# Seven dense layers take gate, up and the next gate together in their first round

## The chip, the cores and the metric

The kernel runs on one core of a Trainium2 chip. A core has a matrix engine (TensorE, PE in the profile, with its weight loads as PEld), VectorE (DVE), ScalarE (ACT), GpSimd (POOL) and SyncE (SP), which issues the loads of weights. The metric is the device time of one execution in microseconds, the median of several runs: 3132.03 us for the kernel before (three runs, 3131.13 to 3134.92).

## The reference, cut to what matters

A model of several kinds of blocks on 256 tokens of 1024 features, with 16 more tokens put in front in one of the blocks. Around the blocks' mixers stand dense layers of this form; the second kind of block has the same gate, up and down without the norm in front, and layer norms behind:

```python
def rmsnorm(x, g):
    xf = x.astype(jnp.float32)
    y = xf * lax.rsqrt(jnp.mean(xf * xf, -1, keepdims=True) + EPS)
    return (y * g.astype(jnp.float32)).astype(x.dtype)

def macaron_half_ffn(x, pre_g, post_g, w_gate, w_up, w_down):
    h = rmsnorm(x, pre_g)
    h = (jax.nn.silu(h @ w_gate) * (h @ w_up)) @ w_down
    return x + 0.5 * rmsnorm(h, post_g)
```

w_gate and w_up are 1024 x 2816, w_down is 2816 x 1024. The change touches the first two products alone.

## The kernel before, in words

x lies with features on the partitions: 8 slices k of 128 features by n tokens. Every operand is split into a high part and a remainder (xh and xl, wh and wl), and a product is three matmuls: xh by wh, xl by wh, xh by wl (`mm3p`, profile lines 594 to 596).

**Weights.** `Mat.get` (lines 222 to 238) brings a block of weights, 1024 rows by 256 columns, in two pieces of 128 x 1024 elements. A piece is loaded on SP's queue into one of 6 raw buffers, cast by ScalarE into one of 5 wh buffers (line 237), and subtracted by VectorE into one of 5 wl buffers (line 238). A buffer comes free when TensorE has done its last matmul with the piece before it. A block makes 48 matmuls: 8 slices k, two halves of 128 columns, three products.

**The dense layer.** `ffn` (line 518 on) splits x (`split_x`, lines 270 and 271, slice by slice as the layer before makes it), and goes through 11 column blocks c. Block c takes a gate block and an up block. For c = 0 both go together, slice by slice, 12 matmuls for each k; later blocks do gate first, then up. With n up to 256, gate c and up c each have one PSUM buffer of the pool `acc`, which has four; so gate 2 takes the buffer of gate 0. `glu` multiplies gate by the norm's factor rb (line 602, VectorE, which reads the gate's buffer for the last time), takes silu on ScalarE (line 603), and multiplies by up (line 607).

**The norm.** As the scale of a token can be applied behind the product, x goes in without it. The squares of x's slices are taken by ScalarE (line 369) and added by GpSimd (line 363). `rms_wide` (lines 396 to 422) is written behind the loops of c = 0: it splits the sum into th and tl, sums over features with two matmuls (lines 410, 411), and makes rb by rw (line 413), a root on ScalarE (line 415), a reciprocal (417) and three small steps (418 to 420). One layer uses the narrow `rms` instead: a sum into columns (line 295), small steps (lines 336 to 343), a broadcast by TensorE (line 325) and a copy to rb (line 394). `by_tokens` (lines 425 to 433) makes a copy of rw's values for the end of the layer (line 429, two matmuls, and line 432).

**The end of a layer.** `add_norm` (line 783) or `layer_norm` (line 860) sums squares over features (line 295), takes the root (`inv_sqrt`, lines 328 to 345, isv to isc), broadcasts it (line 325) and makes the next x slice by slice (t at line 794, x at line 795). `hold_weights` (line 347) keeps the root and its last step in mind; `Mat.get` counts its calls in `held`, and the call at which the count is 0 is issued behind those two. With two calls free, the first four pieces of the next layer (gate 0 and up 0) may go ahead of the root, and the fifth goes behind it.

**What sets the order.** Each engine runs its instructions in its own order, and a scheduler puts them there from the program's order, its dependences and its own estimate of times. So the order on an engine is not the order of the program text; it is shown below where the change moves it.

Seven layers have n up to 256 and no work given as `first`. They are called layers 1 to 7 here, in order of time. Layers 1, 2, 3 and 7 use `rms_wide`; layers 4 and 5, in the second block, have no norm in front; layer 6 uses the narrow `rms`, over 272 tokens.

Of the kernel before, what the change touches and what calls it, by code (L numbers as in the profile page):

```python
# [20 lines left out]
KD = D // 128  # L21
# [150 lines left out]
def parts_tile(p, name, k, n, dtype=F32R, **kw):  # L172

    return p.tile([128, k, (n + 63) // 64 * 64], dtype, name=name, **kw)[:, :, :n]
# [68 lines left out]
class Ops(Net):  # L243
# [274 lines left out]
    def ffn(self, x, n, g, wg, wu, wd, out, first=None, side=None, stats=None):  # L518

        nc = self.nc
        with self.phase("ffn") as p, ExitStack() as scope:
            px = scope.enter_context(self.phase("ffx", side="right"))
            vt = rb = ahead = wide = None
            if first:
                x.need(0)
                parts = []
                for i, (k, m) in enumerate(((0, 2), (2, 2), (4, 4))):
                    parts.append(wg.get(k, m, 0, 256))  # L530
                    x.need(i + 1)
                ahead = [Pieces(2, [t for q in w for t in (q.tiles[0][:, i:i + 2] for i in range(0, q.each, 2))])
                         for w in zip(*parts)]
                first()
            xh, xl = self.split_x(px, x, n, g)
            hh = parts_tile(p, "hh", FF // 128, n)
            hl = parts_tile(p, "hl", FF // 128, n)
            pair = n <= 256

            def tiles(other=0):  # L540
                if pair:
                    t = self.acc.tile([128, 2, 256], F32, name="acc")
                    return t[:, :, :n], [t[:, m, :n] for m in range(2)]
                t = [(self.acc, self.aux)[m < other].tile([128, 512], F32, name=("acc", "aux")[m < other])[:, None, :n]
                     for m in range(2)]
                return t, [a[:, 0] for a in t]

            def mm(ps, w, k):
                for m in range(2):
                    ms = slice(m * 128, m * 128 + 128)  # L550
                    self.mm3p(ps[m], w[0][:, k, ms], w[1][:, k, ms], xh[:, k], xl[:, k],
                              k == 0 and (m == 0 or not pair), k == KD - 1 and (m == 1 or not pair))

            for c in range(FF // 256):
                cg = ahead if ahead and c == 0 else wg.get(0, KD, c * 256, 256)
                cu = wu.get(0, KD, c * 256, 256)
                tg, pg = tiles(2 * (c == 1))
                tu, pu = tiles(c == 1)
                if c == 0 and not first:
                    for k in range(KD):  # L560
                        mm(pg, cg, k)
                        mm(pu, cu, k)
                else:
                    for k in range(KD):
                        mm(pg, cg, k)
                    for k in range(KD):
                        mm(pu, cu, k)
                if c == 0 and g is not None and n == 256 and stats is None:
                    rb, wide = self.rms_wide(p, x, n)
                elif c == 0 and g is not None:  # L570
                    rt, rb, vt = self.rms(x, stats or n)
                    if side:
                        side.stats = rt, rb
                    rb, vt = rb[:, :n], vt[:, :self.nt(n)]
                    if not pair:
                        self.hold_weights(1)
                if pair:
                    self.glu(p, hh[:, 2 * c:2 * c + 2], hl[:, 2 * c:2 * c + 2], tg, tu, rb, n, 2)
                else:
                    for m in range(2):  # L580
                        i = 2 * c + m
                        self.glu(p, hh[:, i:i + 1], hl[:, i:i + 1], tg[m], tu[m], rb, n, 1)
            o = out(hh[:, FF // 128 - 1, 0:1].bitcast(F32))
            self.out_proj(wd, hh, hl, n, list(range(FF // 128)), o, side=side and (lambda: side.place(px)))
            if side:
                side.scope = scope.pop_all()
            if wide is not None:
                vt = self.by_tokens(wide, n, 1e-6)
            return o, vt
# [2008 lines left out]
```

## Time and profile before

| what | value |
|---|---|
| median of three runs | 3132.03 us |
| the profiled execution | 3120.05 us |
| its span | 3117.8 us |
| mean granted clock of TensorE | 0.979 |
| TensorE busy | 3009.0 us, 97% |
| VectorE busy | 2071.4 us, 66% |
| ScalarE busy | 1527.8 us, 49% |
| GpSimd busy | 324.1 us, 10% |

Busy shares are means over the whole span. TensorE's granted clock is given as a share of its full 2.4 GHz: 0.50 is 1.2 GHz. An idle time in brackets behind an instruction is that of its engine just ahead of it, with what ended it. An instruction's times can overlap with the next one's on TensorE, whose matmuls are pipelined: its pace is read from the starts.

### The profile page before, as it was taken

Reading aid. Unit: us, or ns where it says so; the run is one execution under the profiler, and the core shown is the slowest. Engines: PE = TensorE matmul, PEld = TensorE weight load, DVE = VectorE, ACT = ScalarE, POOL = GpSimd, SP = SyncE. Lnnn points to the kernel's source line nnn. Section 1 sums busy time; section 2 is a strip of 40 time slices with the busy share of each in tenths; the row PEclk is TensorE's granted clock in tenths of the full one; section 3 lists DMA queues with packets and bytes.
Section 4 is the critical chain, followed back from the end, with each engine's and each line's share of the span. In section 5 each row is a group of like instructions: output and inputs, shape, how many; then the busy total and the mean of one; then the engine's idle time right before and its main releaser. Section 6 shows DMA issues by size and latency. Waiting matters only on the chain.

```text
span 3117.8 us, 63347 instructions
## 1 busy us (share of the span) xinstructions
PE 3009.0 (97%) x26260; PEld 2899.6 (93%) x26260; DVE 2071.4 (66%) x3465; ACT 1527.8 (49%) x2418; POOL 324.1 (10%) x379
## 2 busy tenths in 40 slices
PE   8999999999899999999999999999999999999998
PEld 8998999999777899999989999999989999998898
DVE  6578766658867765657886665565566656658764
ACT  5455555545433544546565454454444444444543
POOL 0010101000211100001100110100102001012101
PEclk9999999999999999999999999999999999999999
DMA  7664566665311466765345536555443555662453
GB/s 241 192 190 137 167 188 191 203 201 172 103 36 35 123 192 197 208 191 174 112 135 161 171 118 194 180 155 171 142 129 108 172 170 165 193 196 90 130 192 119
DMA packets 142528, 494.61 MB, mean 159 GB/s; under 512 B 15760, under 2 KB 18448, under 8 KB 141984
## 3 DMA queue, kind: packets, MB, share of 16 engines
q1 hardware_dynamic: 136512, 478.88, 49.8%
q10 hardware_dynamic: 5696, 11.62, 1.1%
q8 instruction: 206, 3.38, 0.4%
q14 instruction: 82, 0.67, 0.1%
q0 software_dynamic: 32, 0.07, 0.0%
HBM read 487.35 MB, written 3.15 MB: 157 GB/s over the span
## 4 chain that ended last, share of the span: by engine, by line
PE 90%; DVE 5%; ACT 2%; POOL 2%; issue 1%; DMA 0%; SPq 0%; POOLq 0%; DVEq 0%; ACTq 0%
PE acc L594 25%; PE acc L595 25%; PE acc L596 25%; PE aux L1430 2%; DVE wl L238 1%; PE aux L295 1%; POOL acc L363 1%; PE aux L325 1%; PE acc L2433 1%; ACT wh L237 1%; PE acc L514 1%; PE acc L515 1%; PE acc L516 1%; PE aux L1450 0%; PE aux L668 0%
## 5 line engine op out<-in xcount | busy, mean ns | idle before, releaser
L238 DVE TENSOR_TENSOR wl<-raw,wh 128x1024 fp32r<-128x1024 f32 (+2 forms) x934 | 1123.9, 1207 | 688.4 <-ACT wh L237 679.1
L237 ACT CAST wh<-raw 128x1024 fp32r<-128x1024 f32 (+2 forms) x934 | 952.3, 1023 | 1091.4 <-PE acc L595 802.1
L594 PE MATMUL acc<-xh,wh 128*128 128x256 f32 (+1 forms) x4464 | 1263.8, 285 | 28.9 <-ACT xh L270 17.0
L595 PE MATMUL acc<-xl,wh 128*128 128x256 f32 (+1 forms) x4464 | 1255.1, 282 | 1.3 <-DVE xl L271 1.3
L596 PE MATMUL acc<-xh,wl 128*128 128x256 f32 (+1 forms) x4464 | 1254.8, 281 | 0.9 <-DVE wl L238 0.9
L594 PEld LDWEIGHTS acc<-xh,wh 128*128 128x128 f32 x4464 | 849.6, 191 | 36.7 <-ACT xh L270 18.4
L595 PEld LDWEIGHTS acc<-xl,wh 128*128 128x128 f32 x4464 | 851.7, 191 | 6.5 <-issue 3.6
L596 PEld LDWEIGHTS acc<-xh,wl 128*128 128x128 f32 x4464 | 850.6, 191 | 3.0 <-DVE wl L238 1.3
L594 PE MATMUL acc<-hh,wh 128*128 128x256 f32 (+1 forms) x1760 | 490.2, 279 | 0.0
L596 PE MATMUL acc<-hh,wl 128*128 128x256 f32 (+1 forms) x1760 | 489.8, 278 | 0.0
L595 PE MATMUL acc<-hl,wh 128*128 128x256 f32 (+1 forms) x1760 | 489.8, 278 | 0.0
L595 PEld LDWEIGHTS acc<-hl,wh 128*128 128x128 f32 x1760 | 330.9, 188 | 0.1
L594 PEld LDWEIGHTS acc<-hh,wh 128*128 128x128 f32 x1760 | 330.6, 188 | 0.1
L596 PEld LDWEIGHTS acc<-hh,wl 128*128 128x128 f32 x1760 | 330.6, 188 | 0.0
L363 POOL TENSOR_TENSOR acc<-so 128x256 f32<-128x256 f32 (+1 forms) x16 | 19.6, 1227 | 1120.0 <-ACT so L779 1119.5
L363 POOL TENSOR_TENSOR acc<-acc,so 128x256 f32<-128x256 f32 (+1 forms) x68 | 80.9, 1189 | 305.9 <-ACT so L779 303.1
L607 DVE TENSOR_TENSOR gv<-acc,glu 128x512 f32<-128x512 f32 (+1 forms) x130 | 77.5, 611 | 47.8 <-PE acc L596 42.0
L595 PE MATMUL acc<-ml,wh 128*128 128x256 f32 x280 | 79.8, 287 | 2.3 <-DVE ml L254 2.3
L602 DVE TENSOR_TENSOR glu<-acc,rb 128x512 f32<-128x512 f32 (+1 forms) x106 | 61.3, 596 | 30.4 <-PE acc L596 30.3
L594 PE MATMUL acc<-mh,wh 128*128 128x256 f32 x280 | 80.6, 290 | 0.9 <-ACT mh L1678 0.8
L596 PE MATMUL acc<-mh,wl 128*128 128x256 f32 x280 | 78.9, 284 | 0.0
L609 DVE TENSOR_TENSOR hl<-gv,hh 128x512 fp32r<-128x512 f32 (+1 forms) x132 | 77.2, 602 | 0.0
(620 smaller groups left out, 3772.8 us busy)
## 6 DMA issues: line engine op xcount, KB each, us to landing
raw<-w SPq DMA_DIRECT2D x880, 512.0 KB, 3.9
raw<-w SPq DMA_DIRECT2D x46, 256.0 KB, 3.1
so<-memT ACTq DMA_DIRECT2D x20, 256.0 KB, 3.8
raw<-w SPq DMA_DIRECT2D x8, 192.0 KB, 2.8
x<-xT SPq DMA_DIRECT2D x4, 256.0 KB, 6.1
mk<-so ACTq DMA_DIRECT2D x4, 256.0 KB, 2.5
mv<-so ACTq DMA_DIRECT2D x4, 256.0 KB, 2.9
mk<-mk ACTq DMA_DIRECT2D x1, 1024.0 KB, 4.8
```

Of the source, the lines that this page charges most:

```text
L237: nc.scalar.copy(h, r)
L238: nc.vector.tensor_sub(l, r, h.bitcast(F32))
L295: self.nc.tensor.matmul(ps[:, j:j + 1], a[:, j * 128:(j + 1) * 128], self.tab["ones"], start=(j == 0 and first), stop=(j == nt - 1 and las ...
L325: self.nc.tensor.matmul(ps[:, j * 128:j * 128 + w], r[:w, j:j + 1].to_broadcast([w, 128]), self.tab["ident"][:w, :w], start=(j == 0), stop ...
L363: self.nc.gpsimd.tensor_add(d, total[1], t)
L594: t.matmul(out, wh, xh, start=first, stop=False, **kw)
L595: t.matmul(out, wh, xl, start=False, stop=False, **kw)
L596: t.matmul(out, wl, xh, start=False, stop=last, **kw)
L602: nc.vector.tensor_mul(s, pg, rb[:, None, :].to_broadcast([128, m, n]))
L607: nc.vector.tensor_mul(v, pu, s)
L609: nc.vector.tensor_sub(hl, v, hh.bitcast(F32))
L1430: nc.tensor.matmul(ps[R[a], c], lhsT(c, a), rhs(c, a), start=first and c == 0, stop=c == 3, skip_group_check=True)
```

## The change

In the seven layers the first round takes three weight blocks, gate 0, up 0 and gate 1, slice by slice: 18 matmuls for each k. Their six pieces are asked for by six calls of `get`, each of half a block (four slices), in the order gate 0, up 0, gate 1, and again. The round for c = 1 then has up 1 alone. From c = 2 on nothing changes. Where `held` is 2, it is set to 5, so that five of the small calls may go ahead of the root. `Pieces` puts the two halves of a block together again.

```diff
--- before.py
+++ after.py
@@ -551,12 +551,32 @@
                     self.mm3p(ps[m], w[0][:, k, ms], w[1][:, k, ms], xh[:, k], xl[:, k],
                               k == 0 and (m == 0 or not pair), k == KD - 1 and (m == 1 or not pair))
 
+            three = pair and not first
+            if three and self.held == 2:
+                self.held = 5
             for c in range(FF // 256):
-                cg = ahead if ahead and c == 0 else wg.get(0, KD, c * 256, 256)
-                cu = wu.get(0, KD, c * 256, 256)
-                tg, pg = tiles(2 * (c == 1))
-                tu, pu = tiles(c == 1)
-                if c == 0 and not first:
+                if three and c == 0:
+
+                    each = [(wg, 0), (wu, 0), (wg, 256)]
+                    got = [[w.get(k, 4, at, 256) for w, at in each] for k in (0, 4)]
+                    both = [[Pieces(4, [a[i].tiles[0], b[i].tiles[0]]) for i in range(2)] for a, b in zip(*got)]
+                    (tg, pg), (tu, pu), ahead1 = [tiles() for _ in range(3)]
+                    for k in range(KD):
+                        for w, ps in zip(both, (pg, pu, ahead1[1])):
+                            mm(ps, w, k)
+                elif three and c == 1:
+                    cu = wu.get(0, KD, 256, 256)
+                    (tg, pg), (tu, pu) = ahead1, tiles()
+                    for k in range(KD):
+                        mm(pu, cu, k)
+                else:
+                    cg = ahead if ahead and c == 0 else wg.get(0, KD, c * 256, 256)
+                    cu = wu.get(0, KD, c * 256, 256)
+                    tg, pg = tiles(2 * (c == 1))
+                    tu, pu = tiles(c == 1)
+                if three and c < 2:
+                    pass
+                elif c == 0 and not first:
                     for k in range(KD):
                         mm(pg, cg, k)
                         mm(pu, cu, k)
```

(Lines behind the change have numbers higher by 20: 602 becomes 622, 794 becomes 814.)

**The sum of the norm, TensorE, layer 1.** In these rows acc with a number is a PSUM buffer in use for one block, xh7 is the last slice of x, xh0 the first, th and tl are the sum of squares. Before, the end of up 0 and the start of gate 1:

```order
L594 MATMUL acc_4173<-xh7_4097,wh_4168 128x256
L595 MATMUL acc_4173<-xl7_4105,wh_4168 128x256
L596 MATMUL acc_4173<-xh7_4097,wl_4169 128x256
L410 MATMUL aux_4298<-th_4294,one_4300 128x256 [waits Activation_49]
L411 MATMUL aux_4298<-tl_4295,one_4300 128x256 [waits DVE_49]
L595 MATMUL acc_4344<-xl0_4098,wh_4322 128x256
L596 MATMUL acc_4344<-xh0_4090,wl_4323 128x256
```

After, the end of gate 1 and the start of up 1:

```order
L614 MATMUL acc_4186<-xh7_4097,wh_4180 128x256
L615 MATMUL acc_4186<-xl7_4105,wh_4180 128x256
L616 MATMUL acc_4186<-xh7_4097,wl_4181 128x256
L410 MATMUL aux_4359<-th_4355,one_4361 128x256 [waits Activation_49]
L411 MATMUL aux_4359<-tl_4356,one_4361 128x256 [waits DVE_49]
L614 MATMUL acc_4393<-xh0_4090,wh_4383 128x256
L615 MATMUL acc_4393<-xl0_4098,wh_4383 128x256
```

The two matmuls of lines 410 and 411 stand behind 96 matmuls of the layer before, and behind 144 after. From line 410 to the first matmul of gate 2 there are 97 rows before and 52 after. That place after, the end of up 1 and the start of gate 2:

```order
L614 MATMUL acc_4393<-xh7_4097,wh_4389 128x256
L615 MATMUL acc_4393<-xl7_4105,wh_4389 128x256
L616 MATMUL acc_4393<-xh7_4097,wl_4390 128x256
L429 MATMUL aux_6352<-tab_all_125,rw_4365 128x1 [waits DVE_49]
L429 MATMUL aux_6352<-tab_all_125,rw_4365 128x1
L614 MATMUL acc_4473<-xh0_4090,wh_4451 128x256 [waits DVE_49,PE_49,Activation_49]
L615 MATMUL acc_4473<-xl0_4098,wh_4451 128x256
```

And before:

```order
L594 MATMUL acc_4345<-xh7_4097,wh_4340 128x256
L595 MATMUL acc_4345<-xl7_4105,wh_4340 128x256
L596 MATMUL acc_4345<-xh7_4097,wl_4341 128x256
L594 MATMUL acc_4473<-xh0_4090,wh_4451 128x256 [waits DVE_49,Activation_49]
L595 MATMUL acc_4473<-xl0_4098,wh_4451 128x256
```

Line 429's two matmuls stood at the end of the layer and now stand ahead of gate 2.

**From the sum to the release of gate 0's buffer, VectorE, layer 1.** wl is a weight piece's subtraction; glu is the multiplication by rb. Before:

```order
L254 TENSOR_TENSOR tl<-acc,th 128x256 [waits Activation_49]
L238 TENSOR_TENSOR wl<-raw,wh 128x1024 [waits DMAHW0_49,PE_49,Activation_49]
L413 TENSOR_SCALAR rw<-aux 128x256 [waits PE_49]
L238 TENSOR_TENSOR wl<-raw,wh 128x1024 [waits DMAHW1_49,Activation_49]
L417 RECIPROCAL rb<-t 128x256 [waits Activation_49]
L238 TENSOR_TENSOR wl<-raw,wh 128x1024 [waits DMAHW2_49,PE_49,Activation_49]
L418 TENSOR_TENSOR t<-rb 128x256 [waits DVE_49]
L419 SCALAR_TENSOR_TENSOR t<-t,rw 128x256 [waits DVE_49]
L420 SCALAR_TENSOR_TENSOR rb<-t,rb 128x256 [waits DVE_49]
L238 TENSOR_TENSOR wl<-raw,wh 128x1024 [waits DMAHW3_49,PE_49,Activation_49]
L602 TENSOR_TENSOR glu<-acc,rb 128x512 [waits DVE_49]
```

After:

```order
L238 TENSOR_TENSOR wl<-raw,wh 128x1024 [waits DMAHW1_49,PE_49,Activation_49]
L413 TENSOR_SCALAR rw<-aux 128x256 [waits PE_49]
L238 TENSOR_TENSOR wl<-raw,wh 128x1024 [waits DMAHW2_49,Activation_49]
L417 RECIPROCAL rb<-t 128x256 [waits Activation_49]
L238 TENSOR_TENSOR wl<-raw,wh 128x1024 [waits DMAHW3_49,DVE_49]
L418 TENSOR_TENSOR t<-rb 128x256 [waits DVE_49]
L238 TENSOR_TENSOR wl<-raw,wh 128x1024 [waits DMAHW4_49,PE_49,Activation_49]
L419 SCALAR_TENSOR_TENSOR t<-t,rw 128x256 [waits DVE_49]
L432 TENSOR_SCALAR rv<-aux 128x2 [waits PE_49]
L420 SCALAR_TENSOR_TENSOR rb<-t,rb 128x256 [waits DVE_49]
L238 TENSOR_TENSOR wl<-raw,wh 128x1024 [waits DMAHW5_49,Activation_49]
L622 TENSOR_TENSOR glu<-acc,rb 128x512 [waits DVE_49]
```

Between rw and the multiplication there were three wl; now there are four, and the small rv (line 432). Between tl and rw there are two wl now, of which the second is shown.

**The start, VectorE, layer 1.** o is the output of the layer before, isv to isc its norm's small steps, t the first step of the new x. Before:

```order
L782 COPY o<-acc 128x512 [waits Activation_49]
L782 COPY o<-acc 128x256 [waits Activation_49]
L238 TENSOR_TENSOR wl<-raw,wh 128x1024 [waits DMAHW4_49,PE_49,Activation_49]
L782 COPY o<-acc 128x256 [waits Activation_49]
L336 TENSOR_SCALAR isv<-aux 128x2 [waits PE_49]
L340 RECIPROCAL isy<-isr 128x2 [waits Activation_49]
L341 TENSOR_TENSOR ist<-isy 128x2 [waits DVE_49]
L342 SCALAR_TENSOR_TENSOR ist<-ist,isv 128x2 [waits DVE_49]
L343 SCALAR_TENSOR_TENSOR isc<-ist,isy 128x2 [waits DVE_49]
L238 TENSOR_TENSOR wl<-raw,wh 128x1024 [waits DMAHW5_49,Activation_49]
L794 SCALAR_TENSOR_TENSOR t<-o,vec,aux 128x256 [waits PE_49]
```

After:

```order
L802 COPY o<-acc 128x512 [waits Activation_49]
L802 COPY o<-acc 128x256 [waits Activation_49]
L238 TENSOR_TENSOR wl<-raw,wh 128x1024 [waits DMAHW4_49,PE_49,Activation_49]
L238 TENSOR_TENSOR wl<-raw,wh 128x1024 [waits DMAHW5_49,PE_49,Activation_49]
L802 COPY o<-acc 128x256 [waits Activation_49]
L336 TENSOR_SCALAR isv<-aux 128x2 [waits PE_49]
L340 RECIPROCAL isy<-isr 128x2 [waits Activation_49]
L341 TENSOR_TENSOR ist<-isy 128x2 [waits DVE_49]
L342 SCALAR_TENSOR_TENSOR ist<-ist,isv 128x2 [waits DVE_49]
L343 SCALAR_TENSOR_TENSOR isc<-ist,isy 128x2 [waits DVE_49]
L814 SCALAR_TENSOR_TENSOR t<-o,vec,aux 128x256 [waits PE_49]
```

The fifth wl stood between isc and t, and stands ahead of the last copy of o and of isv.

## Rows read from the trace of the kernel before

**Rows 1.** The page's parts 1 and 4: busy time by engine; the chain by engine.
```profile
PE 3009.0 (97%) x26260; PEld 2899.6 (93%) x26260; DVE 2071.4 (66%) x3465; ACT 1527.8 (49%) x2418; POOL 324.1 (10%) x379
...
PE 90%; DVE 5%; ACT 2%; POOL 2%; issue 1%; DMA 0%; SPq 0%; POOLq 0%; DVEq 0%; ACTq 0%
```

**Rows 2.** Who TensorE waited for: us in total, times, longest us.
```profile
PE acc L594 <- ACT xh L270: 17.0, 8, 2.4
...
PE acc L595 <- DVE xl L271: 1.3, 3, 0.8
...
PE acc L596 <- DVE wl L238: 0.9, 1, 0.9
```

**Rows 3.** Layer 1's start, stretches: us, PE PEld DVE ACT POOL busy, PEclk, DMA, GB/s.
```profile
337.90:343.80 5.90, 5.86 (x27) 5.86 (x28) 5.90 (x15) 3.90 (x11) 3.87 (x4) 0.50 0.18 71
343.80:351.90 8.10, 8.10 (x74) 8.10 (x73) 6.31 (x9) 4.79 (x9) 2.59 (x3) 1.00 0.20 67
```

**Rows 4.** VectorE in order of time, layer 1's start: start us, us, ..., [idle before].
```profile
333.65 0.15 DVE L336 TENSOR_SCALAR isv<-aux 128x2 f32<-128x2 f32 x1
...
335.00 1.23 DVE L238 TENSOR_TENSOR wl<-raw,wh 128x1024 fp32r<-128x1024 f32 x1 [0.18 <-ACT wh L237]
336.14 0.86 DVE L794 SCALAR_TENSOR_TENSOR t<-o,vec,aux 128x256 f32<-128x256 f32 x2
```

**Rows 5.** TensorE in order of time, layer 1.
```profile
334.88 0.71 PE L325 MATMUL aux<-tab_all,isc 128*128 128x128 f32 x4 [1.28 <-DVE isc L343]
...
337.94 0.80 PE L594 MATMUL acc<-xh,wh 128*128 128x256 f32 x2 [2.35 <-ACT xh L270]
...
351.78 0.28 PE L410 MATMUL aux<-th,one 128*128 128x256 f32 x1
```

**Rows 6.** VectorE in order of time, layer 1, from the norm's sum on.
```profile
353.42 0.42 DVE L413 TENSOR_SCALAR rw<-aux 128x256 f32<-128x256 f32 x1
...
354.88 1.75 DVE L417 RECIPROCAL rb<-t 128x256 f32<-128x256 f32 x1
356.55 1.16 DVE L238 TENSOR_TENSOR wl<-raw,wh 128x1024 fp32r<-128x1024 f32 x1
357.63 0.41 DVE L418 TENSOR_TENSOR t<-rb 128x256 f32<-128x256 f32 x1
...
358.54 0.43 DVE L420 SCALAR_TENSOR_TENSOR rb<-t,rb 128x256 f32<-128x256 f32 x1
358.88 1.22 DVE L238 TENSOR_TENSOR wl<-raw,wh 128x1024 fp32r<-128x1024 f32 x1
360.01 1.28 DVE L602 TENSOR_TENSOR glu<-acc,rb 128x512 f32<-128x512 f32 x2
```

**Rows 7.** ScalarE in order of time, layer 1, a cast.
```profile
357.46 1.05 ACT L237 CAST wh<-raw 128x1024 fp32r<-128x1024 f32 x1 [1.71 <-PE acc L595]
```

**Rows 8.** Stretches elsewhere: idle times of TensorE and what follows them.
```profile
1431.20:1434.50 3.30, 0.34 (x4) 0.14 (x2) 2.89 (x6) 2.94 (x6) 0.00 (x0) 1.00 0.72 218
1436.00:1439.40 3.40, 3.24 (x16) 2.94 (x15) 3.29 (x11) 2.76 (x6) 0.00 (x0) 0.51 0.53 157
1486.60:1489.00 2.40, 0.44 (x5) 0.20 (x3) 2.40 (x5) 0.80 (x2) 0.00 (x0) 1.00 0.67 203
1489.00:1493.00 4.00, 3.85 (x33) 3.65 (x33) 3.96 (x10) 1.77 (x3) 0.00 (x0) 1.00 0.47 136
```

**Rows 9.** VectorE in order of time, starts of layers 5 and 7.
```profile
1840.06 1.23 DVE L238 TENSOR_TENSOR wl<-raw,wh 128x1024 fp32r<-128x1024 f32 x1
...
2918.77 0.16 DVE L336 TENSOR_SCALAR isv<-aux 128x2 f32<-128x2 f32 x1 [1.39 <-PE aux L295]
```

**Rows 10.** TensorE and VectorE in order of time, layer 6.
```profile
2627.37 0.83 PE L295 MATMUL aux<-tab_all,acc 128*128 128x1 f32 x6 [0.99 <-POOL acc L363]
...
2630.77 0.93 PE L325 MATMUL aux<-tab_all,isc 128*128 128x128 f32 x6
...
2631.26 2.36 DVE L238 TENSOR_TENSOR wl<-raw,wh 128x1024 fp32r<-128x1024 f32 x2 [1.62 <-ACT wh L237]
```

## The prediction

> **What bounds the kernel now.** I read the page first: TensorE is busy 97% of the span and makes 90% of the chain of waits [rows 1]. So time moves only where TensorE idles or runs at a lower clock; VectorE and ScalarE have room on average. The second view was the list of who waited for whom on TensorE, to see what the change could win at the starts of the seven layers (numbered 1 to 7 in order of time; 1, 2, 3 and 7 take their norm with the wide sum, 6 with the narrow one, 4 and 5 have none). There are 17.0 us of waits for the first slice of x, 8 of them, 1.3 us for its low part, and 0.9 us once for a weight piece [rows 2]. The third was the stretch of layer 1: from its first matmul TensorE is busy 5.86 of 5.90 us at a granted clock of 0.50, and then all of 8.10 us at 1.00 [rows 3]. Nothing starves in the first two blocks there; only the wait ahead of the first matmul and the low clock cost time, and a third block in the round feeds neither. The gain that is there to be had is small. The last view was the order of instructions around the norm, since the change moves that.
>
> **The change part by part.** First the sum of squares. Its two matmuls (lines 410 and 411) stood behind 96 matmuls of gate 0 and up 0, with gate 1 and up 1, 96 matmuls, behind them. Now they stand behind 144, with the 48 of up 1 behind them. The block after that, gate 2, needs the first PSUM buffer, which the VectorE multiplication by rb (line 602) releases. Before: line 410 starts at 351.78 [rows 5], rw at 353.42, the reciprocal at 354.88, rb at 358.54, a weight piece at 358.88, the multiplication at 360.01 [rows 6]; the row there holds two multiplications in 1.28 us, so the first is done at about 360.65: 8.9 us after line 410. TensorE has 96 matmuls at 0.113 us (8.10 us over some 71 of them [rows 3, 5]), 10.9 us, to do meanwhile, so 2 us are to spare.
>
> After: TensorE has only the two matmuls of the sum, 48 of up 1 and two of line 429, about 5.9 us. VectorE has four weight pieces between rw and the release, not three, 1.1 us more as the steps show (356.55 to 357.63 [rows 6]), and the small rv, 0.2 us (isv, of the same shape, takes 0.15 [rows 4]); rw itself can come some 0.5 us sooner after the sum, as no piece that TensorE has yet to free lies directly ahead. That is 8.9 + 1.1 + 0.2 - 0.5 = 9.7 us. The stall is 9.7 - 5.9 = 3.8 us. A second path gives nearly the same from the other side: the last weight piece ahead of the multiplication needs a buffer that up 1 frees with its last matmul, as casts wait for TensorE in rows 7. Behind it come the cast, 1.05 [rows 7], the subtraction, 1.1, and the multiplication, 0.64: 2.8 us with nothing else late. I take 3.7 between 2.8 and 4.2, for layers 1, 2, 3 and 7: 14.8 us (11.2 to 16.8). Behind the waiting multiplication stand only VectorE's own next ones; what is late is gate 2 on TensorE, and nothing later can give it back, since TensorE hardly waits for weights elsewhere [rows 2].
>
> Second, the clock after such an idle time. Before has none inside these layers. Nearest rows: TensorE was busy 0.34 of 3.30 us at 1431.20, and the 3.40 us from 1436.00 ran at 0.51 [rows 8]. On the other side it was busy 0.44 of 2.40 us at 1486.60, and the next 4.00 us stayed at 1.00 [rows 8]. Bounds per stall: nothing, or a stretch like the 5.90 us of rows 3, which costs half, 2.95. I take the row whose idle time is nearest in length, 1431.20: half of 3.40 us, 1.7 each, 6.8 in all (0 to 11.8).
>
> Third, the starts. The fifth weight piece is no longer issued behind the roots of the norm that ends the layer before. In layer 1 it stood at 335.00, 1.23 us, directly ahead of t at 336.14 [rows 4]. Now it stands ahead of isv (333.65) and of the copy of o that line 336's sum needs, so the root chain is some 1.36 us later: the broadcast at 334.88 [rows 5] comes at 336.24, lasts 0.71, and t starts at about 337.0, 0.86 later than now. Layer 3 has the same order: 0.86. In layer 5 the piece of 1840.06 [rows 9] goes between the two small steps of the layer norm; its chain then runs without it behind: 0.8. In layer 6 it goes behind isv: 0.6. Layer 4 waits for its second piece: 0.3. In layer 7 isv waits 1.39 us for TensorE's sum [rows 9], which hides the piece there, and its later place is gone: -0.6. Layer 2's start waits for other work: 0. Sum 2.8 us (1.4 if the low clock at the start ends when it does now, so that only the slow half of the delay is lost; 3.5 if a piece more is late).
>
> Fourth, layer 6's own narrow sum. It stood behind 78 matmuls and waited 0.99 us for GpSimd's squares [rows 10]; behind 144 they are there: -0.99. But its chain (two weight pieces among the small steps now, none between isv and isc before) sends the broadcast, which stood at 2630.77, and the copy, a piece and the multiplication follow, beside 18 matmuls, 2.0 us. Before, a pair of pieces of 2.36 us [rows 10] lay in that place and hid nothing from TensorE. The stall is between 0 and 3 us; I take 1.5, and half a clock drop, 0.85. Together 1.4 (-1.0 to 3.7).
>
> The sum: 14.8 + 6.8 + 2.8 + 1.4 = 25.8 us. The profiled execution took 3120.05 us, 2.25 more than its span of 3117.8, so after would be 3145.9 there; it lies 12 us under the median of the three runs, 3132.03, and the same sum on the median gives 3158.
>
> One rule speaks against the change more loudly than this. Two PSUM buffers take turns every six matmuls in layer 1's first block, and the granted clock is 1.00 throughout the 8.10 us [rows 3]. The Trainium skill, "TensorE: Matmul & The Clock Gate", section "A second HAM failure mode: psum-queue depth-cycling", tells of a kernel whose cycling through PSUM banks made TensorE pause often enough for its clock to swing between the two levels. By the rows three buffers in turn cost nothing; by the rule the longer round would swing too. The same page's section "HAM oscillation — how this bites in real kernels" says that matmuls in bursts with waits between them begin each burst at the low clock; by it the second term is due at each of the four stalls, where rows 8 show one case for and one against.
>
> **The rivals.** (a) The stall without the clock: 19.0 us, 3151. For it 1486.60 in rows 8, against it 1431.20. (b) A longer drop at each stall, 2.95 for 1.7: 30.8, 3163; rows 3 have such a stretch, but after a start whose work is sparse for longer. (c) No stall: up 1's matmuls are late for another reason, or the pieces come so early that VectorE is through in 5.9 us. Then 2.8 - 0.99 = 1.8 remains, 3134. Against it: even without the reciprocal (1.75 us) the chain would be too long [rows 6]. (d) The other side, faster: the first round's extra six matmuls per slice give x time, so the low stretch is shortened. It would have to take half of the 2.95 us that layer 1's stretch loses in all seven layers, -10.3, with 1.3 for the low part of x and 0.99 less, no stall, and 2.8 for the starts: -9.8, 3122. It decides only if TensorE starves in that stretch, and 5.86 of 5.90 us busy speak against it. (e) The swing of the clock through three buffers: 144 matmuls, 16.3 us, at half the clock in seven layers, 114 us, 3246; rows 3 speak against it. That the change does not do what it says is out: the orders show it.
>
> **How the numbers follow.** Forecast 0.52; (a) 0.18; (b) 0.10; (c) 0.10; (d) 0.08; (e) 0.02. A measurement of this kernel tells about 0.2% (6.3 us) from no change. (c) lies within it, (d) is faster, the rest slower: 0.08, 0.10 and 0.82. The likeliest case has its own range, 11.6 (11.2 + 0 + 1.4 - 1.0) to 35.8 (16.8 + 11.8 + 3.5 + 3.7), 3144 to 3168. Downwards the range goes on to (c), 3133; left out are (d), (e) and a little of (b).
>
> **What would show it.** Right: a new wait of TensorE (gate 2's first matmul) for VectorE's multiplication by rb, 4 times about 3.7 us, with a weight subtraction directly ahead of that multiplication; a stretch of about 3.4 us at half the clock behind each; broadcasts at the starts of layers 1 and 3 about 1.4 us later after the last sum; and no wait of line 295 for GpSimd in layer 6. Wrong: no such wait, or one under 2.8 us; the clock at 1.00 behind it; shorter low stretches at the starts.

## The result, and the profile after

The changed kernel took 3167.78 us in the median of four runs (3165.03 to 3176.14), the kernel before 3133.48 in four; the ratio is 1.0114, its 95% interval 1.0090 to 1.0139. That is 34.3 us slower by the medians, where 25.8 had been worked out. The forecast of 3158 stands 10 us below, and 3133.48 by the ratio, 3169.2, lies just above the end of the range. The profiled execution took 3176.14 us, the slowest of the four, with a span of 3174.0: 56 us more than that of before.

The page, busy time by engine and the chain by engine, to be held against [rows 1]:

```profile
PE 3050.1 (96%) x26260; PEld 2941.1 (93%) x26260; DVE 2066.5 (65%) x3465; ACT 1526.1 (48%) x2418; POOL 328.9 (10%) x379
...
PE 88%; DVE 6%; ACT 2%; POOL 2%; issue 1%; DMA 0%; SPq 0%; POOLq 0%; DVEq 0%; ACTq 0%
```

TensorE's busy time is up by 41 us with the same number of matmuls. Who TensorE waited for (us in total, times, longest us), against [rows 2]:

```profile
PE acc L614 <- ACT xh L270: 15.2, 8, 2.0
PE acc L614 <- DVE glu L622: 12.6, 4, 3.2
PE acc L614 <- ACT wh L237: 7.9, 2, 6.7
...
PE acc L616 <- DVE wl L238: 1.2, 2, 0.8
```

The new wait is the one that was forecast: four times, 12.6 us in all, for the multiplication by rb. In layer 1, VectorE in order of time from rw on, against [rows 6]:

```profile
364.77 0.42 DVE L413 TENSOR_SCALAR rw<-aux 128x256 f32<-128x256 f32 x1
...
371.24 1.22 DVE L238 TENSOR_TENSOR wl<-raw,wh 128x1024 fp32r<-128x1024 f32 x1
372.37 1.28 DVE L622 TENSOR_TENSOR glu<-acc,rb 128x512 f32<-128x512 f32 x2
```

And TensorE there, the sum's first matmul and gate 2's first, against [rows 5]:

```profile
363.81 0.28 PE L410 MATMUL aux<-th,one 128*128 128x256 f32 x1
...
373.20 0.35 PE L614 MATMUL acc<-xh,wh 128*128 128x256 f32 x1 [3.22 <-DVE glu L622]
```

From line 410 to the end of the first multiplication (373.01, half of the two in 1.28 us) it takes 9.2 us, where 9.7 were worked out; a piece's subtraction is directly ahead; TensorE waits 3.22. The clock behind it, in stretches of TensorE (length, busy, instructions, granted clock, DMA share, GB/s), against [rows 8]:

```profile
370.10:373.20 3.10, 0.00 (x0) 1.00 0.86 252
374.50:377.90 3.40, 3.40 (x19) 0.50 0.28 113
```

Idle for 3.10 us, and then 3.40 us at 0.50. That is two terms of the sum seen as they were put down.

What the sum did not have is seen in the program's first dense layer, called 0 here, which the change does not touch. First before, then after, 160 us of matmuls without a pause at the full clock:

```profile
30.00:190.00 160.00, 160.00 (x1414) 1.00 0.64 201
```

```profile
30.00:190.00 160.00, 160.00 (x1361) 1.00 0.61 194
351.20:367.20 16.00, 16.00 (x143) 1.00 0.38 119
379.00:395.00 16.00, 16.00 (x138) 1.00 0.56 165
```

There are 1414 matmuls in before and 1361 after: 0.1133 us each in the one, 0.1178 in the other, some 7 us over the layer's 1584. And in layer 1 after, the rows from 351.20 and from 379.00 show the one pace ahead of gate 2 (143 in 16 us) and the other behind it (138). Five of the eight dense layers of the profile after ran at the slow pace for most of their length (0, 1, 2, 4 and 5), none of before.

So I split each layer's length, between two matmuls that are the same in all traces, one near its start and one near its end (in layer 4 they lie inside the layer), into the slow pace (the sum over all distances of 0.115 to 0.125 us between two starts of what they exceed 0.1133) and the rest. The rest repeats within 0.4 us from one run of before to the other, and within 1.7 in the changed kernel, mostly by where the clock falls:

| us, without the slow pace | before | before again | after | after again | forecast of the change |
|---|---|---|---|---|---|
| layer 1 | 204.26 | 204.11 | 210.65 | 208.94 | 6.3 |
| layer 2 | 197.34 | 197.30 | 207.76 | 206.59 | 5.4 |
| layer 3 | 198.54 | 198.53 | 205.20 | 205.91 | 6.3 |
| layer 4 | 172.67 | 172.66 | 172.56 | 172.73 | 0.3 |
| layer 5 | 189.40 | 189.26 | 189.84 | 189.95 | 0.8 |
| layer 6 | 201.39 | 201.31 | 201.15 | 201.12 | 2.0 |
| layer 7 | 197.43 | 197.04 | 202.49 | 201.93 | 4.8 |
| change, sum of the seven | | -0.8 | +28.6 | +26.1 | 25.8 |
| slow pace in layers 0 to 7 | 1.5 | 29.3 | 34.8 | 10.0 | |

(The columns "again" are from the first two experiments. The forecast gives 3.7 for the stall, 1.7 for the clock and the start's term.) The change costs 26 to 29 us, and most of what else differs from run to run is the pace. It is not all: for the profile after, the table gives 28.6 + 33.3 = 61.9 us, where the spans differ by 56.2. The parts between the dense layers vary too; the one between layers 0 and 1 took 133, 138, 132 and 134 us in the four profiles, in the table's order.

### The profile page after: what moved, and what is told of

The parts are those of the page before. It is cut to its first block, busy times and chain, and to the rows that moved or that the text cites. A ratio compares the mean times of both kernels' runs of the same rounds, so it can differ in the third digit from the quotient of the medians.

```text
span 3174.0 us, 63348 instructions
## 1 busy us (share of the span) xinstructions
PE 3050.1 (96%) x26260; PEld 2941.1 (93%) x26260; DVE 2066.5 (65%) x3465; ACT 1526.1 (48%) x2418; POOL 328.9 (10%) x379
## 4 chain that ended last, share of the span: by engine, by line
PE 88%; DVE 6%; ACT 2%; POOL 2%; issue 1%; DMA 0%; SPq 0%; POOLq 0%; DVEq 0%; ACTq 0%
PE acc L614 25%; PE acc L615 25%; PE acc L616 25%; PE aux L1450 2%; DVE wl L238 1%; PE aux L325 1%; PE aux L295 1%; POOL acc L363 1%; PE acc L2453 1%; ACT wh L237 1%; PE acc L514 1%; PE acc L515 1%; PE acc L516 1%; PE aux L1470 0%; DVE t L814 0%
## 5 line engine op out<-in xcount | busy, mean ns | idle before, releaser
L615 PE MATMUL acc<-xl,wh 128*128 128x256 f32 (+1 forms) x4464 | 1268.7, 285 | 1.4 <-DVE xl L271 1.4
L616 PE MATMUL acc<-xh,wl 128*128 128x256 f32 (+1 forms) x4464 | 1268.3, 284 | 1.2 <-DVE wl L238 1.2
L616 PEld LDWEIGHTS acc<-xh,wl 128*128 128x128 f32 x4464 | 860.0, 193 | 3.7 <-DVE wl L238 1.9
L622 DVE TENSOR_TENSOR glu<-acc,rb 128x512 f32<-128x512 f32 (+1 forms) x106 | 61.2, 596 | 33.4 <-PE acc L616 33.3
```

Source lines behind the costliest of these rows:

```text
L615: t.matmul(out, wh, xl, start=False, stop=False, **kw)
L616: t.matmul(out, wl, xh, start=False, stop=last, **kw)
L622: nc.vector.tensor_mul(s, pg, rb[:, None, :].to_broadcast([128, m, n]))
```

## The experiments

Theory A: the change costs what the table shows, and the pace is drawn anew at a break of TensorE's even run (a wait, or other work in between), in any kernel. Theory B: the change sets the pace.

**1. The kernel before again**, no edit.

> The kernel before once more, unchanged. In its first profile all nine long layers ran their matmuls 0.1133 us apart; in the profile of the changed kernel five of them, layer 0 among them, which the change does not touch, ran 0.1178 apart, 6.7 us each, 33 us in all. Theory A: each pause of TensorE draws one of the two paces, in any kernel, so this profile shows some layers at 0.1178 (two of nine would fit the 12 us by which the median lies over the first profile), and its times spread by multiples of some 6.7 us, 3120 to 3145. Theory B: the change causes the slow pace; then no long layer here runs at 0.1178 and the ratio to before is 1.000 within 0.2%.

Median 3136.78 us of 12 runs, 3117.03 to 3146.59; ratio 0.9996 (0.9977 to 1.0015). Layers 1, 4, 5 and 7 were at the slow pace in the profile, 0 was not (the first row is of layer 0, the second of layer 1):

```profile
30.00:190.00 160.00, 160.00 (x1414) 1.00 0.65 200
352.00:368.00 16.00, 16.00 (x138) 1.00 0.64 189
```

Theory B falls: a kernel without the change has a slow pace in four layers, and its runs spread over 30 us.

**2. The changed kernel again**, no edit.

> The changed kernel once more, unchanged. Theory A (the pace is drawn anew in each run): other layers than 0, 1, 2, 4 and 5 are slow, or another number of them; the waits for the multiplication (12.6 us, four times) and the low clock behind them (about 2 us each) stay as they are, and a run without slow layers would take about 3143. Theory B (the change sets it): the same five layers are slow again and the time is 3165 to 3176.

Median 3155.80 of 7 runs (3150.73 to 3163.60), ratio 1.0062 (1.0040 to 1.0083). Layer 0 was slow, and layer 1 up to gate 2; layers 2, 4 and 5 were not:

```profile
30.00:190.00 160.00, 160.00 (x1361) 1.00 0.61 193
352.00:368.00 16.00, 16.00 (x139) 1.00 0.39 115
379.00:395.00 16.00, 16.00 (x144) 1.00 0.56 165
```

In layer 1 the pace changes at the same place as in the first profile, the other way round. The wait for the multiplication is there again, as long and as often:

```profile
PE acc L614 <- DVE glu L622: 12.6, 4, 3.2
```

The two ratios of one kernel have intervals that do not meet; of the 11 runs of both, the median is 3161.7. So an interval from a few runs is too narrow for a spread like this. All four of the first runs lie above all seven of these, which would happen once in 330 times if each run drew for itself; that runs taken together share something is a rival that no run here tests.

**3. Gate 2 in the other pool.**

> The changed kernel, with gate 2 in a PSUM buffer of the other pool, so that it need not wait for the multiplication that releases gate 0's. Theory A: the four waits (12.6 us) and the low clock behind them (2.0 to 4.3 us each) go, some 20 us less than the changed kernel at equal paces, which leaves before plus 3 to 8; slow layers still turn up. Theory B (the wait sets the slow pace of the layer, as in layers 1 and 2): the slow pace of layers 1 and 2 goes too, 13 us more. Rival to both: the wait moves to up 2, which now takes gate 0's buffer 5.4 us later; then less than 5 us are won.

```diff
-                    tg, pg = tiles(2 * (c == 1))
+                    if three and c == 2:
+                        t = self.aux.tile([128, 512], F32, name="aux").rearrange("p (m n) -> p m n", m=2)
+                        tg, pg = t[:, :, :n], [t[:, m, :n] for m in range(2)]
+                    else:
+                        tg, pg = tiles(2 * (c == 1))
```

Median 3143.73 of 12, ratio 1.0020 (1.0001 to 1.0038). TensorE's waits in the products of the dense layers:

```profile
PE acc L618 <- ACT wh L237: 8.4, 3, 6.7
...
PE acc L620 <- DVE wl L238: 1.7, 2, 1.0
```

The wait for the multiplication is gone, and no other has come for it. Without the slow pace the seven layers are 7.1 us above before, 19 to 22 less than the changed kernel: the 20 that were expected. The stall and its clock are the main cost. What stays is 4.2 in layer 2 and about 2 each in layers 3 and 5. Only layer 5 was at the slow pace. That layers 1 and 2 were not says nothing for the expectation's theory B: with the wait in place, in experiment 2, they were not either, but for the first part of layer 1.

**4. Four calls ahead of the root.**

> The changed kernel with four small calls free ahead of the root, not five: the fifth weight piece is behind the root again, as before. If the third term of the sum holds (2.8 us over the starts of layers 1, 3, 5, 6 and 7), the waits at the starts shrink by 1 to 3 us and nothing else moves; if the starts are set by something else, no change. By times the difference is too small to tell beside the slow pace; the profile tells it: the start of layer 1's first matmul after the last sum of the layer ahead, 0.8 us sooner than in the changed kernel.

```diff
-                self.held = 5
+                self.held = 4
```

Median 3159.52 of 6, ratio 1.0067 (1.0044 to 1.0090). Layer 1's start, the last sum of the norm ahead, the broadcast and the first product:

```profile
331.35 1.24 PE L295 MATMUL aux<-tab_all,acc 128*128 128x1 f32 x8
333.86 0.85 PE L325 MATMUL aux<-tab_all,isc 128*128 128x128 f32 x4 [1.27 <-DVE isc L343]
336.93 1.01 PE L614 MATMUL acc<-xh,wh 128*128 128x256 f32 x3 [2.22 <-ACT xh L270]
```

From the sum to the first product it is 5.58 us, 3.07 of it behind the broadcast (3.06 in [rows 5]); in the changed kernel it is 6.93 (its rows stand in the next section), 1.35 more. Without the slow pace the seven layers are 23.9 above before, 2 to 5 less than the changed kernel; 2.8 were worked out. The term holds in size, not closer than that.

**5. Both undone** (the edits of 3 and 4).

> The changed kernel with gate 2 in the other PSUM pool and four small calls free ahead of the root: both costs of the change undone, the rounds of 18 matmuls kept. If the sum has its terms right, wait and low clock come back to those of before within 2 us (32.4 and 17.4 us in the eight dense layers of the first profile), with layer 6's 0.99 us less; the time is that of before within 0.2%. If the longer round were worth something by itself, this would be faster than before by more than 0.2%; if a third cost were missed, slower.

Median 3132.91 of 12, ratio 1.0002 (0.9981 to 1.0022). Without the slow pace: layer 2 +4.5, layer 6 -1.3, the other five within 0.3, +3.2 in all. The long rounds by themselves give nothing but the 1 us in layer 6, and there was a third cost, in layer 2.

**6. The stall filled.**

> The changed kernel with 28 matmuls more, of th by the ones, behind up 1 in layers 1, 2, 3 and 7, written to a buffer that nobody reads: TensorE is busy for the 3.2 us in which it waits for the multiplication. If the idle time makes the clock fall, the low clock of these layers (15 to 20 us in three profiles of the changed kernel, 8.9 in before) comes back to about 9 to 10, and the time is 6 to 10 us less than the changed kernel at equal paces, the 12.6 us of waits still being spent. If the clock falls for another reason, wait goes into work and nothing is won. And if a pause draws the pace anew, these layers keep one pace from start to end, where the changed kernel changed it at gate 2 in layers 1 and 2.

```diff
+                    if wide is not None:
+                        idle = self.aux.tile([128, 512], F32, name="aux")[:, :n]
+                        for _ in range(28):
+                            nc.tensor.matmul(idle, self.spare[0], self.spare[1], start=True, stop=True)
```

Median 3157.06 of 6, ratio 1.0079 (1.0056 to 1.0102). Layer 1:

```profile
360.92 3.34 PE L576 MATMUL aux<-th,one 128*128 128x256 f32 x28
364.64 0.36 PE L619 MATMUL acc<-xh,wh 128*128 128x256 f32 x1 [0.39 <-DVE glu L627]
```

And stretches: layer 1 behind the filling, layer 3 ahead of it and behind it:

```profile
364.60:368.00 3.40, 3.36 (x29) 1.00 0.72 276
1070.00:1086.00 16.00, 16.00 (x143) 1.00 0.61 174
1094.00:1110.00 16.00, 16.00 (x138) 1.00 0.65 194
```

The clock stays at 1.00 behind all four. Without the slow pace the seven layers are 20.8 above before, 5 to 8 less than the changed kernel: the idle time makes the clock fall, and the fall costs 1.3 to 2.0 us a layer. The last sentence of the expectation failed: in layer 3 the pace goes from 143 to 138 matmuls in 16 us across the filled place. A wait of 0.39 us is left there, as in layer 1's row above, so this run does not tell whether the wait or the matmuls with other operands let it change.

**7 and 8. The starts filled**, in the kernel before and in the one with both undone.

> The kernel before, with 4 matmuls more behind the last sum of a layer's norm and 7 behind the broadcast of its factor, to a buffer that nobody reads: TensorE has work in the 1.3 and 2.4 us in which it waits ahead of the layers that end with this norm. If these waits cost the clock, the low clock at the starts of layers 1, 2, 3, 6 and 7 (about 12 of 17.4 us) goes in part; the slices of x, which come every 1.3 us, would then be late for rounds of 12 matmuls (1.36 us), so some of it turns into waits for x: 4 to 9 us less than before. If the low clock stays, no change, or a few us more for the added work.

> The kernel with both costs undone, with the same filling at the starts. Rounds of 18 matmuls (2.04 us at the full clock) are longer than a slice of x takes, so there should be no wait for x even at the full clock: 2 to 5 us less than the filled before, 8 to 12 less than before. If rounds of 12 are not short of x either, the two filled kernels are alike within 2 us in wait and clock.

```diff
         ss = s.tok_sum([self.total[0], self.last], n)
+        idle = s.aux.tile([128, 512], F32, name="aux")
+        for _ in range(4):
+            nc.tensor.matmul(idle[:, :128], self.last[:, :128], s.tab["ident"], start=True, stop=True)
...
         cb = s.bcast(c, n)
+        idle = s.aux.tile([128, 512], F32, name="aux")
+        for _ in range(7):
+            nc.tensor.matmul(idle[:, :128], c[:, :1].to_broadcast([128, 128]), s.tab["ident"], start=True, stop=True)
```

Medians 3130.27 and 3134.09 of 12 each, ratios 1.0001 (0.9980 to 1.0021) and 1.0016 (0.9995 to 1.0037). Waits of number 7:

```profile
PE aux L295 <- POOL acc L363: 5.0, 4, 2.3
...
PE acc L595 <- DVE xl L271: 2.6, 4, 0.9
```

The low clock goes at the starts of layers 1, 2, 3 and 7, but the seven layers of number 7 are 3.4 us above before without the slow pace (1 to 5 by where a layer is taken to begin and end, since the filling makes their ends longer too): layer 1 wins 1.3, layers 2, 4 and 6 lose 1.4 to 2.0, layer 0's end 1.5. Waits for GpSimd's sums (3.2 us in before, 3 times) and for xl (1.3 [rows 2]) come up, and the filling itself seems to delay where the next work needs TensorE at once, which was not tried apart. Number 8 wins 2.0 in layer 1, 2.1 in layer 6 and 1.1 in layer 7, and has layer 2's loss of 5.6. So rounds of 18 do somewhat better at the full clock, in layers 1 and 6, by 0.7 and 3.5 us; both kernels missed what was expected of their times.

**9. The cast of th behind that of the sixth piece**, on top of number 5. Layer 2's third cost, in the changed kernel's profile: TensorE in the middle of gate 1, then ScalarE:

```profile
560.87 0.38 PE L614 MATMUL acc<-xh,wh 128*128 128x256 f32 x1 [1.23 <-ACT wh L237]
...
562.13 0.52 PE L616 MATMUL acc<-xh,wl 128*128 128x256 f32 x1 [0.76 <-DVE wl L238]
```

```profile
559.47 0.41 ACT L253 CAST th<-acc 128x256 fp32r<-128x256 f32 x1 [3.81 <-POOL acc L363]
559.78 2.94 ACT L237 CAST wh<-raw 128x1024 fp32r<-128x1024 f32 x3
```

TensorE waits 1.23 us for a cast that stands behind th, which waits 3.81 us for GpSimd's sum of squares, and 0.76 for its subtraction.

> The kernel with both costs undone, and the cast of th put behind the cast of the sixth weight piece. In layer 2 the changed kernel and the one with both costs undone wait 1.2 us for that cast and 0.8 for its subtraction, in the middle of gate 1, and run 3.4 us at half the clock behind it; on ScalarE the cast stands behind that of th, which waits for the last sum of squares. If that order is the cause, both waits and the low clock go and layer 2 takes, its slow pace taken out, 197.3 us as before, not 201.6; the other layers stay. If it is the fewer pieces ahead of the root (one small call free, where it was one whole call), the wait stays, at least 1 us.

```diff
-        self.split(th, tl, total[0][:, :n])
+        with self.tc.issue_after(self.cast.ins):
+            self.split(th, tl, total[0][:, :n])
```

(`self.cast` is the last cast that `Mat.get` issued.) Median 3133.21 of 12, ratio 1.0006 (0.9991 to 1.0022). The same place, ScalarE and then TensorE:

```profile
544.21 1.05 ACT L237 CAST wh<-raw 128x1024 fp32r<-128x1024 f32 x1 [1.08 <-PE acc L620]
546.95 0.41 ACT L253 CAST th<-acc 128x256 fp32r<-128x256 f32 x1 [1.69 <-POOL acc L363]
547.26 1.99 ACT L237 CAST wh<-raw 128x1024 fp32r<-128x1024 f32 x2
```

```profile
548.05 0.39 PE L621 MATMUL acc<-xh,wl 128*128 128x256 f32 x1 [0.70 <-DVE wl L238]
```

The wait for the cast is gone and the low clock too; 0.70 for the subtraction stays. Layer 2 is 198.60, 3.2 of the 4.5 given back; the seven layers together are where before has them (0.0). The order on ScalarE was the cause of most of it; what the last 1.3 are was not tried.

**10. The starts filled where a dense layer follows**, with number 9: the matmuls of 7 behind five norms, those ahead of layers 1, 3, 6 and 7 and of one of the two larger dense layers (272 tokens), which the expectation does not name.

> The same with the filling of the starts, only behind the norms that are followed by layers 1, 3, 6 and 7. Against before, the slow pace taken out: layer 1 -2, layer 2 0, layer 3 0, layer 6 -2, layer 7 -1, as in the filled kernel with rounds of 18, and nothing lost at the ends of layer 0 and of others, where that kernel lost 1.2 to 1.8 each. That makes 5 us less than before, 0.16%, which times cannot tell (five rounds tell 0.2%) but the layers' own stretches can. If rounds of 12 would do as well at the full clock, the change's rounds are worth nothing even there.

Median 3124.59 of 12, ratio 0.9977 (0.9955 to 0.9999): faster than both kernels, than the one before by 0.2% with an interval that just excludes none, and by experiment 2 such an interval can be too narrow. Layer 1's start and the stretch that ran at 0.50 in [rows 3]:

```profile
338.69 0.71 PE L325 MATMUL aux<-tab_all,isc 128*128 128x128 f32 x4 [0.28 <-DVE isc L343]
339.23 1.73 PE L822 MATMUL aux<-tab_all,isc 128*128 128x128 f32 x14
341.75 0.61 PE L619 MATMUL acc<-xh,wh 128*128 128x256 f32 x3 [0.79 <-ACT xh L270]
```

```profile
344.00:349.90 5.90, 5.90 (x54) 1.00 0.01 3
```

Without the slow pace the seven layers are 6.2 us under before: layer 1 -1.7, layer 2 +0.9, layer 6 -3.4, layer 7 -1.4, the others within 0.5. The kernel of number 9, without the filling, stands at 0.0 there, so with rounds of 18 the filling gives it. What it would give to the kernel before behind the same norms alone was not run; number 7 fills behind all of them.

## Why the prediction was right or wrong

**The stall: right.** 12.6 us for 14.8, at gate 2, with the multiplication behind a subtraction. The half microsecond a layer that I had too much is in part VectorE's start: rw came 0.96 us after line 410, not 1.1. Of the two paths that had been worked out, VectorE's chain was the later: the last piece's cast, at 369.61 on ScalarE, was done at 370.65, and its subtraction came at 371.24, behind the last step of rb.

**The clock behind it: right in kind and size.** Filled, the stall gives 5 to 8 us back where 6.8 were put down. In layer 1 the first 1.3 us behind the wait still ran at 1.00 (373.20 to 374.50); in layer 2 gate 2 began at 0.50. Of the two rules of the Trainium skill, "TensorE: Matmul & The Clock Gate", the trace agrees with the section "HAM oscillation — how this bites in real kernels" in that the clock fell behind each wait (0.50 behind 3.10 us without work, in rows above), but in layer 1 the burst did not begin at the low clock; of what "A second HAM failure mode: psum-queue depth-cycling" tells no run here shows anything: with three buffers in turn the granted clock was 1.00 from 351.20 on, as with two.

**The starts: right by and large.** In layer 1 of the changed kernel the fifth piece stands ahead of isv, and t directly behind the broadcast, as worked out (VectorE, then TensorE):

```profile
338.78 1.22 DVE L238 TENSOR_TENSOR wl<-raw,wh 128x1024 fp32r<-128x1024 f32 x1 [0.18 <-ACT wh L237]
...
340.26 0.15 DVE L336 TENSOR_SCALAR isv<-aux 128x2 f32<-128x2 f32 x1
...
342.74 0.87 DVE L814 SCALAR_TENSOR_TENSOR t<-o,vec,aux 128x256 f32<-128x256 f32 x2 [1.31 <-PE aux L325]
```

```profile
337.62 0.50 PE L295 MATMUL aux<-tab_all,acc 128*128 128x1 f32 x4
339.09 0.61 PE L295 MATMUL aux<-tab_all,acc 128*128 128x1 f32 x4 [0.96 <-ACT acc L796]
341.49 1.22 PE L325 MATMUL aux<-tab_all,isc 128*128 128x128 f32 x4 [1.79 <-DVE isc L343]
344.55 0.80 PE L614 MATMUL acc<-xh,wh 128*128 128x256 f32 x2 [1.84 <-ACT xh L270]
```

The last sum waits 0.96 us in its middle for the square that stands behind the fifth cast on ScalarE; it is this square that it needs, not the copy of o that the prediction named. The broadcast comes 1.35 us later behind the sum than before (1.4 had been put down), and runs in the low clock now, 1.22 us for 0.71, which I had not put in: the first product comes 1.35 us later, for 0.86. The starts together are 2 to 5 us by experiment 4, where 2.8 were put down. "Layer 2's start waits for other work: 0" is the term that failed here. The first product does start as it did; but with one small call ahead of the root, where it had been one whole call, the sixth piece's cast fell behind th on ScalarE, and the middle of gate 1 waited: 4.2 to 4.5 us with its clock. The order of ScalarE around th would have shown it; I had looked at that in layer 1 alone and taken it for the other three.

**Layer 6: the stall did not come.** 1.4 and 0.6 were put down, and -0.2 was measured. The sum and the broadcast:

```profile
2685.75 0.72 PE L295 MATMUL aux<-tab_all,acc 128*128 128x1 f32 x6
...
2690.07 0.93 PE L325 MATMUL aux<-tab_all,isc 128*128 128x128 f32 x6
```

Neither waits. On VectorE the chain from isv to rt runs from 2686.64 to 2689.86, 3.2 us, and the 32 matmuls between the two (3.6 us) are enough; the GpSimd wait of 0.99 is gone, as forecast. The two misses, 4.3 and -2.2, partly cancel; that the sum of the terms came out so near is in part luck.

**The pace: the term that the sum lacked.** The step that failed for the time as a whole is the last one, from the profiled execution to the median. The sum was made on an execution without a single slow layer, "12 us under the median", and I carried those 12 us over as if they were a constant of the run, with nothing for them in the range. About two slow layers of some 7 us would make them; the runs of that median have no trace to show it. The one of the first four runs of the changed kernel that has a trace lost 34.8 us to the pace, where the profile before lost 1.5; the other three have none. What is drawn in a kernel's runs then belongs in the range: 30 us between the fastest and the slowest run of before. Seen over all runs, 26 to 29 us of change stand against 25.8; the single medians, +34.3 and +19.8, lie on both sides of it, and the first is 8.5 us above it. Nor does a measurement of this kernel tell 0.2% from no change, as the prediction had it: two of the changed kernel differ by 0.5%.

**Open.** What draws the pace. Of 96 dense layers in twelve profiles, 22 were slow for most of their length, 6 of 16 in the changed kernel's two and 16 of 80 in the other ten; that the change makes it more frequent is neither shown nor excluded. That the first four runs were slower than the next seven is put down to it, but those runs have no trace, apart from the first of each set, and what runs taken together may share (experiment 2) was not tried.

## What to carry to other kernels

When more work is put ahead of a reduction, count what is left between the reduction and the first consumer of what it releases: here 96 matmuls had hidden a chain of 9 us, and 50 did not. On an engine that runs in its order a piece put ahead of a release can become a wait, so look at that order in each instance, not in one. And before a forecast of 1%, ask why two executions of the same kernel differ by 0.4%, and take the answer's spread into the range.

## What the runs showed of the hardware that was not expected

TensorE's even run of 128x256 matmuls, each with its own weight load, has two paces at the full granted clock of 1.00: 0.1133 and 0.1178 us from start to start. A pace can last for a whole layer, and a dense layer at the slow one takes 6 to 7 us more. In the twelve profiles the pace changed nearly always where the run was broken. It changed at waits, of 0.22 us in layer 1 of experiment 8 (350 us) and longer ones elsewhere. It changed at a few other matmuls without a wait: in layer 6 of experiment 2 it was 0.1133 up to line 295 at 2667 us, 0.1178 for the 31 matmuls up to line 325 at 2672, and 0.1133 again. A stretch at half the clock kept it in layer 1 of the first profile after (0.1178 on both sides, 374 to 378 us) but not in layer 3 of experiment 4 (0.1178 for nine matmuls from 1091 us, 0.1133 behind the low stretch). In layer 2 of experiments 2 and 4 it changed once (at 548 and 538 us) where the records show neither a wait nor other matmuls.

The clock fell to 1.2 GHz at each of the twelve stalls of 2.9 to 3.2 us in the changed kernel's two profiles and in experiment 4's, for 3.4 us in ten and 6.8 in two. Shorter idle times went either way: in the kernel before, 1.96 us ahead of 530.0 was followed by 0.50 from 531.5 on, and 1.96 us ahead of 1488.9 by 1.00.
